# Gates turned to rows by a transpose, transposes of the rows in four later steps, and held weights at the last token blocks

## The chip, the cores and the metric

The kernel runs on one core of a Trainium2 chip. The core has a matrix engine (TensorE, PE in the profile; PEld is its weight load), VectorE (DVE), ScalarE (ACT), GpSimd (POOL) and SyncE (SP), which here does nothing but issue transfers. Every transfer of this kernel goes through the one queue that SP issues to. The metric is the time of one execution on the device in microseconds; the time shown is a median of several runs.

## The reference

The input is x, 512 tokens by 2048 features, float32, and a conditioning vector c. Two layers follow each other. Both are sandwich-normalised and modulated: for each layer `mod = silu(c) @ ada_w + ada_b` is split into shift, scale and gate, and the layer adds `gate * rmsnorm(y, g_post)` to the stream.

- Layer one is an mLSTM mixer with 8 heads (key width 256, value width 512): one input product `h @ w_in` gives queries, keys, values, an output gate o and a gate z; queries and keys go through a causal convolution of width 4; the head's output is normalised, multiplied with `sigmoid(o)` and `silu(z)`, and goes through `w_out` (4096 to 2048).
- From the residual stream after layer one, with its own norm and modulation (`kv_ada_w`), one shared set of keys and values is made: `kv = hkv @ kv_w`.
- Layer two is a band attention with 16 heads of width 128 and a relative-position bias. Its queries and a gate z come from `h @ b_w_in`; its output goes through `b_w_out` (2048 to 2048).

```
mod = sc @ ada_w[l] + ada_b[l]
shift, scale, gate = mod[:, :D], mod[:, D:2*D], mod[:, 2*D:]
h = modulate(rmsnorm(x, g_pre[l]), shift, scale)
...
x = x + gate[:, None, :] * rmsnorm(y, g_post[l])
```

## The kernel before

**Products.** Every large product is done in three matmuls on two halves of each operand: a float32 value is split into a rounded high part and the rest (`split`, L152: ScalarE casts the high part, L153; VectorE subtracts, L154). `mm3` (L176) issues high by high, high by low and low by high. Weights come as a stream of pieces in a fixed order (`wpiece`, L158): SP loads a raw piece of up to 512 KB (L167), then ScalarE and VectorE split it. Raw, high and low pieces have three buffers each, and this work has a priority `AHEAD` over what the program says at that place, so the planner puts it ahead of other work on each engine. `proj_a` (L192) keeps the weights stationary; `proj_b` (L195) keeps the tokens stationary, with two 128-row slices of 512 weight columns in a piece, for up to four blocks of 128 tokens: 24 matmuls a piece with four blocks, 12 with two. Sums lie in PSUM, five buffers for the large products (`newp`) and three for small ones (`newa`).

**Order.** A planner orders the instructions of each engine from the order of the program and its priorities. The loads and sums of the modulation are pinned to the program's order.

**Modulation.** `mod` has 128 columns of 128 values. Each column is two loads of 512 KB (`ada_load`, L236) and two multiply-and-sum instructions on VectorE (`ada_sum`, L240). The first 64 halves are done at the start, for what layer one needs first. The other 192 are done beside the heads: `background` (L401) sums the three halves that are loaded and then loads the next three, since there are three buffers. It is called in each head after the second and fourth of the query and key products (q1, q3), halfway through and behind the value product (vm, v), after the second and fourth o product (o1, o3), the same for z (z1, z3), and at the head's end; head 0 makes three of these calls, head 1 leaves the q calls out. What is left is summed after the last head.

**Layer one's end.** The gates (`gate` times the post-norm weight) are made as columns in `ggate` and stored to a scratch buffer `ggd` in one transfer (L538). `gate_row` (L567) reads 512 gate values of it, spread over all partitions, into the one buffer `gb`, which shares its memory with a buffer that the heads use. Each head leaves its normalised rows in the scratch buffer `ysc` by four stores (L526); `y_tile` loads them (L557, `yr`) and splits them for the output product. `rows` (L640) does that product: first column group 0 for all four token blocks, then groups 1 to 3 for the pair of blocks 0 and 1, then groups 1 to 3 for blocks 2 and 3. `evac` (L571) multiplies with the gate row and sums squares.

**Residual and transposes.** For each token block, `residual` (L583) finishes the post-norm, adds x, sums squares again and stores the rows; `turned` (L604) scales the rows by the new norm (`xn`, L613), transposes them in 128 by 128 blocks on TensorE (`ps_x`, L621), eight for a column group of a pair, keeps them (ScalarE, a store), and for the second pair makes the key inputs at once (`key_input`, L594). The first pair's residual and transposes happen in `rows(1, (2, 3))`; the second pair's come right after the last `rows`, at high priority, ahead of the value products `values` (L663).

```
with tc.high_priority(AHEAD):
    residual(2)
    residual(3)
    turned(1, True)
```

**Layer two's end.** The output product `b_w_out` takes three column groups with all four token blocks, then the last group for blocks 0 and 1, then for blocks 2 and 3 (L806 to L815). `finish` (L799) makes a block's norm factor, four final products (L803) and four stores (L804); blocks 0 and 1 finish during the last pair's product, blocks 2 and 3 after it.

Of the kernel before, what the change touches and what calls it, by code (L numbers as in the profile page):

```python
# [15 lines left out]
P = 128  # L16
D = 2048
S = 512
# [87 lines left out]
def hybrid_trunk(ctx, tc, xT, xN, c, adaT, cols, wst, wg, ext, kc, out):  # L106
# [88 lines left out]
    def proj_b(mat, xs, pss, midway=None, ms=range(4), kts=KT, at={}):  # L195

        for k0 in range(0, kts, 2):
            if midway and k0 == kts // 2:
                midway()
            if k0 in at:  # L200
                at[k0]()
            hi, lo = wpiece(mat)
            for j in range(2):
                k = k0 + j
                x = xs(k) if callable(xs) else xs[k]
                w = slice(j * 512, (j + 1) * 512)
                for ps, m in zip(pss, ms):
                    t = slice(m * P, (m + 1) * P)
                    mm3(ps, x[:, 0, t], x[:, 1, t], hi[:, w], lo[:, w], k == 0, k == kts - 1)
# [191 lines left out]
    def background(h=NH, where=""):  # L401

        if h == 0 and where not in ("vm", "v", "end") or h == 1 and where[0] == "q":
            return
# [5 lines left out]
        del pending[:ADA_BUFS]  # L410

    for h in range(NH):
# [27 lines left out]
        proj_b("a_w_in", h1, pv, lambda: background(h, "vm"))  # L440
# [86 lines left out]
        if h < NH - 1:  # L527
            background(h, "end")
    while loaded or pending:
        background()  # L530
    for k in range(KT):
        amul_col(KT + k, 96 + KT + k, KVG + k)
        amul_col(2 * KT + k, 48 + KT + k, GPRE + KT + k)
    nc.vector.tensor_tensor(ggate[:, :KT], mod[:, 2 * KT : 3 * KT], cl[:, GPOST : GPOST + KT], op=ALU.mult)
    nc.vector.tensor_tensor(
        ggate[:, KT:], mod[:, 48 + 2 * KT : 48 + 3 * KT], cl[:, GPOST + KT : GPOST + 2 * KT], op=ALU.mult
    )
    nc.sync.dma_start(ggd.rearrange("l k p -> p (l k)"), ggate)  # L538
# [44 lines left out]
    def residual(m):  # L583
        rs = row_rstd(m)
        for g in range(4):
# [6 lines left out]
            nc.sync.dma_start(xsc[m, :, d], y)  # L592

# [10 lines left out]
    def turned(pair, use):  # L604
# [3 lines left out]
        rs = [row_rstd(m) for m in ms]  # L608
        for g in range(4):
            xn = []  # L610
            for i, m in enumerate(ms):
                n = tp.tile([P, S], F32, tag="t", name=f"xn{m}_{g}")
                nc.vector.tensor_scalar(n, yt[m][g], rs[i], None, op0=ALU.mult)  # L613
# [36 lines left out]
    for pair, ms in enumerate(PAIRS):  # L650
        for g in range(1, 4):
            at = {}
            if pair == 1 and g == 1:
                at = {2: lambda: residual(0), 4: lambda: residual(1), 12: lambda: turned(0, False)}
# [15 lines left out]
    with tc.high_priority(AHEAD):  # L670
        residual(2)
        residual(3)
        turned(1, True)
    for ms in PAIRS:
        for g in range(2):
            values(g, ms)
# [129 lines left out]
    for g in range(4):  # L806
        gate_row(1, g)
        for pair in [range(4)] if g < 3 else PAIRS:
            ps = [newp(f"ps_y1_{g}_{m}") for m in pair]
            at = {4: lambda: finish(0), 6: lambda: finish(1)} if pair == PAIRS[1] else {}  # L810
            proj_b("b_w_out", y2, ps, ms=pair, at=at)
# [64 lines left out]
```

## Time and profile before

| | |
|---|---|
| median of 3 runs | 2883.31 us (2882.78 to 2885.15) |
| the profiled execution's own time | 2881.31 us |
| its span, first to last instruction | 2879.5 us |
| mean granted TensorE clock | 0.996 |
| data moved | 491.09 MB, mean 171 GB/s |
| weight loads of 512 KB | 520, median 3.3 us from issue to landing |
| modulation loads of 512 KB | 256, 5.6 us |
| loads of normalised rows (yr) | 16, 5.1 us |
| gate store `ggd<-ggate`, 16 KB | 1, 17.1 us |
| gate read-backs `ssum<-ggd`, 256 KB | 11, 3.5 us |

The span is that of the profiled execution; 1.81 us of its time lie around the span. Busy shares count the time in which an engine worked; a TensorE that is busy 99% can still start its matmuls further apart than the shortest pitch. A line of waits names the engine and the operation that waited, what released it, the sum of the waits, their number and the longest one. In a timeline the columns are the start, the length, the engine, the line, the operation and, in brackets, the idle time before it and what ended it. A granted clock of 1.00 is full speed; at half of it a 512-column matmul takes nearly twice as long.

### The profile page before, as it was taken

How to read it: one execution, taken by the hardware profiler on the slowest of the kernel's cores; microseconds unless marked ns; L12 is line 12 of the kernel's file. 1: busy time of each engine (PE TensorE's matmuls, PEld its weight loads, DVE VectorE, ACT ScalarE, POOL GpSimd, SP SyncE). 2: the span in 40 equal slices, each digit the busy share in tenths (PEclk: the TensorE clock that was granted, in tenths of full speed). 3: DMA queues.
4: the chain of work that ended last, by engine and by line, in shares of the span. 5: the costliest groups of instructions: out<-in, count | busy, mean ns of one | idle time of the engine just before them, and what ended most of it. 6: DMA issues, size and time to landing. Idle time of an engine off the chain costs nothing.

```text
span 2879.5 us, 33007 instructions
## 1 busy us (share of the span) xinstructions
PE 2839.1 (99%) x12768; PEld 2343.9 (81%) x12768; DVE 1587.6 (55%) x2358; ACT 1122.6 (39%) x1642; POOL 0.2 (0%) x4
## 2 busy tenths in 40 slices
PE   8999999999999999999999999999999999999998
PEld 5887888888888888888888788878888888888886
DVE  7985846475374664754646445575222455545425
ACT  4244534334242342422433345464222455545323
POOL 0000000000000000000000000000000000000000
PEclk9999999999999999999999999999999999999999
DMA  8874546455465454554546757686222322222334
GB/s 301 313 242 151 191 153 202 160 181 191 140 202 174 164 186 160 171 195 148 197 156 232 174 194 237 222 271 219 100 95 99 136 91 92 88 92 89 135 106 168
DMA packets 158998, 491.09 MB, mean 171 GB/s; under 512 B 21092, under 2 KB 30180, under 8 KB 158328
## 3 DMA queue, kind: packets, MB, share of 16 engines
q1 hardware_dynamic: 158840, 488.98, 50.5%
q8 instruction: 100, 1.64, 0.2%
q14 instruction: 58, 0.48, 0.0%
HBM read 467.89 MB, written 26.26 MB: 172 GB/s over the span
## 4 chain that ended last, share of the span: by engine, by line
PE 93%; DMA 3%; DVE 2%; ACT 1%; issue 1%; SPq 0%; DVEq 0%; ACTq 0%
PE ps_z L174 17%; PE ps_y L174 16%; PE ps_o L174 12%; PE ps_v L174 12%; PE ps_qk L174 9%; PE ps_q L174 6%; PE ps_k L174 6%; PE ps_kv L174 5%; PE ps_l L174 3%; PE ps_s L174 2%; PE ps_lead L174 2%; PE ps_n L174 2%; DMA yr<-ysc 1%; DVE wl L154 1%; PE ps_t L744 1%; DMA ada<-in_adaT 1%
## 5 line engine op out<-in xcount | busy, mean ns | idle before, releaser
L154 DVE TENSOR_TENSOR wl<-wr,wh 128x1024 fp32r<-128x1024 f32 (+3 forms) x586 | 680.3, 1162 | 1107.1 <-ACT wh L153 1106.5
L153 ACT CAST wh<-wr 128x1024 fp32r<-128x1024 f32 (+3 forms) x586 | 587.6, 1003 | 1439.1 <-PE ps_y L174 230.3
L174 PE MATMUL ps_y<-wh,y 128*128 128x512 f32 x1536 | 476.7, 391 | 7.1 <-ACT y L153 6.7
L174 PE MATMUL ps_z<-h,wh 128*128 128x512 f32 x1408 | 433.8, 389 | 0.0
L174 PEld LDWEIGHTS ps_y<-wh,y 128*128 128x128 f32 x1536 | 289.1, 189 | 68.1 <-ACT y L153 7.5
L174 PE MATMUL ps_v<-wh,h 128*128 128x512 f32 x1024 | 317.2, 389 | 0.0
L174 PEld LDWEIGHTS ps_z<-h,wh 128*128 128x128 f32 x1408 | 263.4, 188 | 54.0
L174 PE MATMUL ps_y<-wl,y 128*128 128x512 f32 x768 | 300.3, 391 | 0.0
L174 PE MATMUL ps_o<-h,wh 128*128 128x512 f32 x896 | 276.3, 389 | 0.0
L174 PE MATMUL ps_z<-h,wl 128*128 128x512 f32 x704 | 274.1, 389 | 0.0
L174 PE MATMUL ps_qk<-h,wh 128*128 128x512 f32 x768 | 237.7, 391 | 0.0
L174 PEld LDWEIGHTS ps_v<-wh,h 128*128 128x128 f32 x1024 | 192.1, 188 | 39.8
L174 PE MATMUL ps_v<-wl,h 128*128 128x512 f32 x512 | 199.5, 390 | 0.0
L174 PEld LDWEIGHTS ps_o<-h,wh 128*128 128x128 f32 x896 | 167.5, 188 | 34.3
L174 PE MATMUL ps_o<-h,wl 128*128 128x512 f32 x448 | 174.5, 389 | 0.0
L240 DVE CUSTOM_DVE_ANT_0 ada<-ada,scB,cl 128x1024 f32<-128x1024 f32 x128 | 163.9, 1281 | 13.4 <-DMA ada<-in_adaT 13.3
L240 DVE CUSTOM_DVE_ANT_0 ada<-ada,scB,mod 128x1024 f32<-128x1024 f32 x128 | 164.1, 1282 | 11.6 <-DMA ada<-in_adaT 10.2
L174 PEld LDWEIGHTS ps_y<-wl,y 128*128 128x128 f32 x768 | 144.8, 189 | 29.9
L174 PEld LDWEIGHTS ps_qk<-h,wh 128*128 128x128 f32 x768 | 143.3, 188 | 29.0
L174 PE MATMUL ps_kv<-wh,hkv 128*128 128x512 f32 x512 | 160.3, 393 | 0.0
L174 PE MATMUL ps_q<-h,wh 128*128 128x512 f32 x512 | 159.3, 392 | 0.0
L174 PE MATMUL ps_k<-hkv,wh 128*128 128x512 f32 x512 | 157.7, 389 | 0.0
(214 smaller groups left out, 3388.8 us busy)
## 6 DMA issues: line engine op xcount, KB each, us to landing
wr<-in_wst SPq DMA_DIRECT2D x520, 512.0 KB, 3.3
ada<-in_adaT SPq DMA_DIRECT2D x256, 512.0 KB, 5.6
yr<-ysc SPq DMA_DIRECT2D x16, 512.0 KB, 5.1
wr<-in_wst SPq DMA_DIRECT2D x30, 256.0 KB, 4.1
ysc<-so SPq DMA_DIRECT2D x28, 256.0 KB, 5.6
wr<-in_wst SPq DMA_DIRECT2D x16, 384.0 KB, 5.7
bsc<-in_ext SPq DMA_DIRECT2D x16, 320.0 KB, 5.8
xt<-in_xT SPq DMA_DIRECT2D x4, 1024.0 KB, 6.9
```

The lines of the kernel that those rows point to most:

```text
L153: nc.scalar.copy(hi, src)
L154: nc.vector.tensor_tensor(lo, src, hi.bitcast(F32), op=ALU.subtract)
L174: nc.tensor.matmul(ps, a, b, start=start, stop=stop)
L240: pin(nc.vector.tensor_tensor_reduce(at, at, scB[:, j * D // 2 : (j + 1) * D // 2], 1.0, mod[:, i : i + 1] if j else col(CB + i), ALU.mult ...
L744: nc.tensor.transpose(ps[:, P * (i - j) : P * (i - j + 1)], pr[i][:, P * j : P * (j + 1)], ident)
```

## The change

It has four parts.

1. `background` is called at pieces 4 and 10 of the value product instead of at piece 8. Head 0 uses one of the two (v4); head 1 leaves out q1, q3 and v4; the last head leaves out o3, z1 and z3. By the instruction order, heads 2 to 6 issue 30 loads each (27 before), the last head 15 (27 before), and no modulation load or sum is left after it.
2. `gates_out(layer)` replaces the one store of all gates. It multiplies the layer's 16 gate columns, transposes them on TensorE to 16 rows of 128 values, copies these on ScalarE, and stores rows of 512 bytes. Layer one's gates go out after head 3, layer two's after the last head.
3. `proj_b` goes through its last piece token block by token block, where before each 128-row slice went through all blocks. With `late=3`, which only the very last product has, the last three pieces are held; block 2 goes through all three, and then block 3.
4. `residual` ends with the new norm's factor, which was the start of `turned`. `turned` takes a list of column groups. For the first pair they are placed at pieces k = 16, 20, 24 and 28 of `rows(1, (2, 3))` (all four at 12 before); for the second pair at k = 0, 4, 8 and 12 of the second value product, at that place's own priority (all four ahead of the first value product at high priority before).

```diff
@@ -192,21 +192,26 @@
     def proj_a(mat, xs, ps, t0=0, t1=S):
         proj(mat, xs, [ps], 8, 0, len(xs), len(xs) - 1, t0, t1)
 
-    def proj_b(mat, xs, pss, midway=None, ms=range(4), kts=KT, at={}):
-
+    def proj_b(mat, xs, pss, ms=range(4), kts=KT, at={}, late=0):
+
+
+        held = []
         for k0 in range(0, kts, 2):
-            if midway and k0 == kts // 2:
-                midway()
             if k0 in at:
                 at[k0]()
-            hi, lo = wpiece(mat)
-            for j in range(2):
-                k = k0 + j
-                x = xs(k) if callable(xs) else xs[k]
-                w = slice(j * 512, (j + 1) * 512)
-                for ps, m in zip(pss, ms):
-                    t = slice(m * P, (m + 1) * P)
-                    mm3(ps, x[:, 0, t], x[:, 1, t], hi[:, w], lo[:, w], k == 0, k == kts - 1)
+            held.append((k0, *wpiece(mat)))
+            if k0 >= kts - 2 * late and k0 < kts - 2:
+                continue
+            for group in [[pm] for pm in zip(pss, ms)] if k0 == kts - 2 else [list(zip(pss, ms))]:
+                for ka, hi, lo in held:
+                    for j in range(2):
+                        k = ka + j
+                        x = xs(k) if callable(xs) else xs[k]
+                        w = slice(j * 512, (j + 1) * 512)
+                        for ps, m in group:
+                            t = slice(m * P, (m + 1) * P)
+                            mm3(ps, x[:, 0, t], x[:, 1, t], hi[:, w], lo[:, w], k == 0, k == kts - 1)
+            held.clear()
 
     def newp(name):
         return psP.tile([P, S], F32, tag="p", name=name)
@@ -400,7 +405,9 @@
 
     def background(h=NH, where=""):
 
-        if h == 0 and where not in ("vm", "v", "end") or h == 1 and where[0] == "q":
+        if h == 0 and where not in ("v4", "v", "end") or h == 1 and where in ("q1", "q3", "v4"):
+            return
+        if h == NH - 1 and where in ("o3", "z1", "z3"):
             return
         for a in loaded:
             ada_sum(*a, tc.keep_in_program_order)
@@ -408,6 +415,17 @@
         for i, j in pending[:ADA_BUFS]:
             loaded.append(ada_load(i, j, ap_, ADA_BUFS, tc.keep_in_program_order))
         del pending[:ADA_BUFS]
+
+    def gates_out(layer):
+
+        gg = ggate[:, layer * KT : (layer + 1) * KT]
+        c0 = 48 * layer + 2 * KT
+        nc.vector.tensor_tensor(gg, mod[:, c0 : c0 + KT], cl[:, GPOST + layer * KT : GPOST + (layer + 1) * KT], op=ALU.mult)
+        ps = newa(f"ps_gg{layer}")
+        nc.tensor.transpose(ps[:KT, :P], gg, ident)
+        row = tp.tile([P, S], F32, tag="t", name=f"gg{layer}")[:KT, :P]
+        nc.scalar.copy(row, ps[:KT, :P])
+        nc.sync.dma_start(ggd[layer], row)
 
     for h in range(NH):
         for i in (2 * h, 2 * h + 1):
@@ -437,7 +455,7 @@
             nmd, nm.rearrange("p (a b) -> p a b", a=4), maskd.unsqueeze(1).to_broadcast([P, 4, P]), op=ALU.add
         )
         pv = [newp(f"ps_v{h}_{m}") for m in range(4)]
-        proj_b("a_w_in", h1, pv, lambda: background(h, "vm"))
+        proj_b("a_w_in", h1, pv, at={k: lambda k=k: background(h, f"v{k}") for k in (4, 10)})
         v = []
         for m in range(4):
             if m < 3:
@@ -526,16 +544,14 @@
             nc.sync.dma_start(ysc[h, :, i, :], so[i])
         if h < NH - 1:
             background(h, "end")
+        if h == 3:
+            gates_out(0)
     while loaded or pending:
         background()
     for k in range(KT):
         amul_col(KT + k, 96 + KT + k, KVG + k)
         amul_col(2 * KT + k, 48 + KT + k, GPRE + KT + k)
-    nc.vector.tensor_tensor(ggate[:, :KT], mod[:, 2 * KT : 3 * KT], cl[:, GPOST : GPOST + KT], op=ALU.mult)
-    nc.vector.tensor_tensor(
-        ggate[:, KT:], mod[:, 48 + 2 * KT : 48 + 3 * KT], cl[:, GPOST + KT : GPOST + 2 * KT], op=ALU.mult
-    )
-    nc.sync.dma_start(ggd.rearrange("l k p -> p (l k)"), ggate)
+    gates_out(1)
     hst.close()
     phA.close()
 
@@ -590,6 +606,7 @@
             nc.vector.scalar_tensor_tensor(y, y, rs, xr, op0=ALU.mult, op1=ALU.add)
             nc.scalar.activation(newa(f"sqx{m}_{g}"), y, AF.Square, accum_out=ssq[:, 4 * m + g : 4 * m + g + 1])
             nc.sync.dma_start(xsc[m, :, d], y)
+        row_rstd(m)
 
     def key_input(k, tmp, t):
 
@@ -601,16 +618,15 @@
             hkv.append(xp.tile([P, 2, S], F32R, tag="x", name=f"hkv{k}"))
         split(hkv[k][:, 0, t], hkv[k][:, 1, t], tmp)
 
-    def turned(pair, use):
+    def turned(pair, gs, use):
 
         ms = PAIRS[pair]
         t = slice(2 * P * pair, 2 * P * (pair + 1))
-        rs = [row_rstd(m) for m in ms]
-        for g in range(4):
+        for g in gs:
             xn = []
             for i, m in enumerate(ms):
                 n = tp.tile([P, S], F32, tag="t", name=f"xn{m}_{g}")
-                nc.vector.tensor_scalar(n, yt[m][g], rs[i], None, op0=ALU.mult)
+                nc.vector.tensor_scalar(n, yt[m][g], rsn[:, m : m + 1], None, op0=ALU.mult)
                 xn.append(n)
             for kk in range(2):
                 k = 4 * g + 2 * kk
@@ -651,7 +667,8 @@
         for g in range(1, 4):
             at = {}
             if pair == 1 and g == 1:
-                at = {2: lambda: residual(0), 4: lambda: residual(1), 12: lambda: turned(0, False)}
+                at = {2: lambda: residual(0), 4: lambda: residual(1)}
+                at |= {16 + 4 * i: lambda i=i: turned(0, [i], False) for i in range(4)}
             if pair == 1 and g == 3:
                 at = {k: lambda k=k: [key_input(i, kept(i, slice(0, 2 * P)), slice(0, 2 * P)) for i in range(k // 2 - 1, k // 2 + 1)] for k in range(2, 32, 4)}
             gate_row(0, g)
@@ -670,10 +687,10 @@
     with tc.high_priority(AHEAD):
         residual(2)
         residual(3)
-        turned(1, True)
-    for ms in PAIRS:
+    for pair, ms in enumerate(PAIRS):
         for g in range(2):
-            values(g, ms)
+            turn = {4 * i: lambda i=i: turned(1, [i], True) for i in range(4)} if pair == 0 and g == 1 else {}
+            values(g, ms, turn)
     for i in range(KT):
         ps = newp(f"ps_k{i}")
         proj_a("kv_w", hkv, ps)
@@ -808,7 +825,7 @@
         for pair in [range(4)] if g < 3 else PAIRS:
             ps = [newp(f"ps_y1_{g}_{m}") for m in pair]
             at = {4: lambda: finish(0), 6: lambda: finish(1)} if pair == PAIRS[1] else {}
-            proj_b("b_w_out", y2, ps, ms=pair, at=at)
+            proj_b("b_w_out", y2, ps, ms=pair, at=at, late=3 if pair == PAIRS[1] else 0)
             with tc.high_priority(AHEAD):
                 for p, m in zip(ps, pair):
                     yo[m].append(op.tile([P, S], F32, tag="o", name=f"yo{m}_{g}"))
```

## The prediction

> **What bounds the kernel now.** I read the busy shares and the clock row of the page first, then the waits of TensorE over the whole span, then the waits and the timeline of the SP queue around the two longest of them, and last the tail.
>
> ```profile
> PE 2839.1 (99%) x12768; PEld 2343.9 (81%) x12768; DVE 1587.6 (55%) x2358; ACT 1122.6 (39%) x1642; POOL 0.2 (0%) x4
> ```
> ```profile
> PE ps_lead L174 <- ACT h L219: 6.8, 3, 3.4
> PE ps_y L174 <- ACT y L153: 6.7, 1, 6.7
> ...
> PE ps_x L621 <- DVE xn L613: 3.5, 4, 1.3
> ...
> PE ps_q L174 <- ACT sp_q L153: 1.8, 1, 1.8
> ...
> PE ps_kv L174 <- DVE wl L154: 0.8, 1, 0.8
> ```
>
> TensorE is the bound: at full clock one 512-column matmul starts every 0.2267 us, and nearly all the span is that pitch. What an edit can win is the time in which matmul starts lie further apart. Counted from the starts, that is 35.5 us in the first 80 us (not touched), 13.0 between 1530 and 1640 (A, the first token product with the output weights), 3.9 between 1780 and 1820 (B, transposes of pair 0), 7.8 between 1915 and 1960 (C, transposes of pair 1), about 14 in the attention stage, and about 1 per mLSTM head, where no wait of TensorE is listed at all. Behind the last matmul there is a tail (D) of 11.1 us.
>
> A, the SP queue's waits between 1500 and 1700, its timeline, and the windows (columns: length, busy of PE, PEld, DVE, ACT, POOL, granted clock, DMA share, GB/s):
>
> ```profile
> SPq L569 <- DMA ggd<-ggate: 10.9, 1, 10.9
> ```
> ```profile
> 1592.42 0.43 SPq L538 DMA_DIRECT2D ggd<-ggate  x1
> ...
> 1598.19 0.33 SPq L167 DMA_DIRECT2D wr<-in_wst  x1
> 1609.51 0.32 SPq L569 DMA_DIRECT2D ssum<-ggd  x1
> 1609.92 0.38 SPq L557 DMA_DIRECT2D yr<-ysc  x1
> ```
> ```profile
> 1606.00:1613.00 7.00, 0.45 (x2) 0.03 (x1) 0.00 (x0) 0.51 (x1) 0.00 (x0) 0.86 0.72 120
> 1613.00:1618.00 5.00, 4.84 (x12) 3.78 (x13) 3.81 (x5) 3.03 (x6) 0.00 (x0) 0.51 0.78 275
> 1926.00:1932.00 6.00, 4.70 (x27) 3.71 (x26) 5.64 (x12) 3.93 (x7) 0.00 (x0) 1.00 0.88 290
> 1932.00:1938.00 6.00, 4.86 (x25) 3.23 (x23) 4.87 (x12) 5.93 (x18) 0.00 (x0) 1.00 0.42 146
> 1938.00:1942.00 4.00, 3.34 (x8) 2.67 (x9) 4.00 (x8) 1.76 (x5) 0.00 (x0) 0.59 0.78 257
> ```
>
> The gates go out in 4-byte elements: issued at 1592.42, landed 17.1 us later. Their read-back stands in the one queue in use and waits 10.9 us; the next load of normalised head rows (yr) stands behind it at 1609.92, and TensorE starves at 1606. After that gap the clock is 0.51. The last two rows show half clock at C too, behind the transposes.
>
> D, the tail:
>
> ```profile
> 2867.77 1.37 DVE L572 TENSOR_TENSOR yo<-ps_y,ssum 128x512 f32<-128x512 f32 x2 [5.17 <-PE ps_y L174]
> ...
> 2868.02 0.39 PE L174 MATMUL ps_y<-wh,y 128*128 128x512 f32 x1
> ...
> 2870.27 2.74 DVE L803 SCALAR_TENSOR_TENSOR yo<-yo,rsn,x 128x512 f32<-128x512 f32 x4
> ...
> 2873.12 2.74 DVE L803 SCALAR_TENSOR_TENSOR yo<-yo,rsn,x 128x512 f32<-128x512 f32 x4
> ```
>
> Both last token blocks end together, so eight final products of 0.67 us stand in a row on VectorE behind the last matmul.
>
> **Part by part, against the profiled run: 2881.31 us, of which 2879.5 span; the median of the runs is 2.0 above it.**
>
> *Gates by rows, and modulation sums moved (A).* Removed from A: the store in 4-byte pieces, and six modulation sums (1.28 us each) with their loads that now stand between 1567 and 1588 among the head rows' splits. In the changed kernel all 256 loads are issued and summed before the last head's rows go out: heads 2 to 6 carry 30 instead of 27, the last 15 instead of 27. Layer 0's gates leave after head 3, some 700 us before their read, which then waits only for the last use of the buffer, about 1539.7. In the queue's new order the read stands ahead of the last head's four stores; layer 1's store stands next to it, waits for a transpose and a copy (about 1546.4), and holds the queue until then; the first normalised store is then ready at about 1555 and the weight load behind it is needed at 1577, so 20 us cover it. If that cover went, a store as slow as today's (17.1) would just be absorbed.
> What goes, from the starts of the matmuls: the wait for the sum of squares 1.9 (no sums between the norm's steps on VectorE), 0.9 near 1589, 6.9 at 1606, 0.4 behind it, and ten matmuls at 0.427 instead of 0.227, 2.0: together 12.1. The new transpose of the gates, its copy and a shorter wait ahead of the norm's sum stay: 0.4. Bounds: 12.1 if nothing stays; if the queue's hold until 1546.4 starves TensorE as the 1606 wait did, 12.1 less 6.9 less 2.0 = 3.2. I take 11.7, near the upper end, since the walk through the rows finds 20 us of cover.
> The Trainium skill ("DMA: Bandwidth & Descriptors", Specifications) says that transfers under 512 bytes get less than the line rate, with a read-modify-write; the trace's 17.1 us for 16 KB agrees, beside 3.5 us for the 256 KB read-back. By that rule alone the new 512-byte rows would leave at line rate, and the sum would be the same.
>
> *More modulation work per head (2 to 6).* Three more loads and sums each: 3 x 1.28 = 3.8 us of VectorE, busy 732.5 of 1268 us there, and 1.5 MB, where DMA has a share of 0.52. Product v now has calls at two places instead of one. Hidden by the weight pieces held ahead: a sum waiting for its load delays the next piece's subtract, but the buffers hold a piece of 5.44 us more. In the trace of before sums wait 11 times in the heads, 2.5 us at most, and TensorE never does. Without the cover each late load costs its excess over 5.44; the slowest modulation load took 12.3. Bounds: -1 (the heads' small gaps close) to +2.5 (half a microsecond in each of five heads); I take 0, the value in the trace of before.
>
> *Transposes of pair 0 spread over four places (B).* Today three waits of 0.33, 0.29 and 1.37 = 2.0. Each group of eight (1.04 us) now has some 24 matmuls = 5.4 us ahead of it for two products of 0.48 on VectorE. The first stands at the same place as today and keeps about 0.3: gain 1.7, between 0 and 2.0.
>
> *Transposes of pair 1 inside the second value product (C).* Today waits of 1.46, 0.94, 0.85 and three short ones = 3.8, then eight matmuls at half clock, 1.6. The rest (2.4) is transposes and changes of shape, and stays. In the changed order TensorE has 24 matmuls between groups: 5.44 + 1.04 = 6.48 us a round. VectorE needs two xn (0.95), four scalings and four subtracts (3.0) and two weight subtracts (2.3): 6.24 a round. That is tight. Bounds: 5.4 if nothing waits; if each of four groups waits as long as the longest today (4 x 1.46 = 5.8), -0.4. It fits by 0.2 a round, with pieces prepared ahead, so I take 1.0 of new waits: gain 4.4.
>
> *Tail (D).* The last three pieces are held; block 2's 18 matmuls go first, so block 2 is complete 18 x 0.2267 = 4.1 us before the end. Its final products end at E+0.8 (E: end of the last matmul), then for block 3 come evacuation 0.7, square and read 0.8, reduce, root and reciprocal 0.8, four products 2.74, with gaps: the last ends at E+5.65, today at 2875.86 = E+7.45. Gain 1.8. Held buffers: piece 14's cast can start when piece 8 frees them (2860.09 in today's times), its two halves need 2.5 us, and block 2 reaches it at 2862.8: a margin of 0.2. Bounds: 2.5 if block 3 evacuates ahead of block 2's products, -0.7 if the piece is late by its own 2.5 us.
>
> Sum: 11.7 + 0 + 1.7 + 4.4 + 1.8 = 19.6. 2881.3 - 19.6 = 2861.7; with 2.0, a median of 2863.7.
>
> **Rivals.** (1) *VectorE becomes the bound in C and the shapes of B keep their waits*: A and D alone, 13.5, time 2869.8. For it: 5.64 of 6.00 us busy in the window from 1926. Against: that window also holds the residual sums, which are over before the new place.
> (2) *Transposes in groups stop the clock*: half clock came at 1938 after 12 us in which transposes and waits of 1.5 at most were mixed with matmuls. Were each of the eight groups followed by eight matmuls at half clock (1.6 each, 12.8, where today 1.6 is paid), the sum would be 19.6 - 12.8 = 6.8: 2876.5. Against: the 32 transposes of B show 1.00 throughout, and 1.04 us is shorter than any stretch that brought half clock here. The Trainium skill ("TensorE: Matmul & The Clock Gate", Part 4) says transposes do not count as work for the gate; C's half clock agrees, B's full clock shows a group alone is not enough.
> (3) *Slower: the sums in product v starve TensorE.* From the call ahead of product v to the first one in it, 10.9 us (two pieces) lie between loads and sums where there were 21.8; if loads land late, VectorE stands in order before the weight subtracts. It must cost 19.6 / 5 = 3.9 us a head to cancel all, and 5.1 a head for slower by 0.2%: 2863.7 + 5 x 5.1 = 2889.2. That takes a sum about 10 us late, past the 5.44 of cover. Against it, 2.5 us is the longest seen there.
> (4) *The change doesn't do what it says* (the planner draws the transposes together again): the instruction order shows them apart, so only a runtime wait could undo it; it falls in with (1).
>
> **How the numbers follow.** Forecast within its own bounds (2860 to 2868): 0.61. Rival 1 and partial forms of it: 0.18 (2868 to 2872). Rival 2: 0.07, just faster in 0.03 of it and the same in 0.04. Rival 3: 0.10, of which 0.03 stays within 0.2% and 0.07 is slower. Gains beyond my terms: 0.04. The range reaches from 2859 (12.1 + 1 + 2.0 + 5.4 + 2.5 = 23.0 would be 2860.3, a little run difference below) to 2872. 0.2% (5.8 us) is about what a measurement tells from no change here: faster 0.61 + 0.18 + 0.04 + 0.03 = 0.86, same 0.07, slower 0.07.
>
> **What would show it.** Right: no wait of the queue at the gate's read; waits of TensorE between 1530 and 1640 under 1.5 us, clock 1.00 there; waits before ps_x under 1.5 in all; last matmul to span end 9.3 us; no wait listed in the heads. Wrong: gaps of TensorE in product v of heads 2 to 6; half clock behind each group of transposes; a wait for the piece held last, about 4 us before the end.

## The result, and the profile after

The changed kernel takes 2863.37 us (median of 4 runs, 2862.53 to 2863.64) against 2883.05 of the kernel before (4 runs): ratio 0.993, with a 95% interval of 0.9913 to 0.9948, so a gain of 0.7% that is clear of no change. The forecast was 2863.7. The profiled execution took 2862.53 us with a span of 2860.7, so its span is 18.8 us shorter than before.

The first lines of the page, and TensorE's waits over the whole span (engine, operation, releaser: sum, number, longest):

```profile
PE 2832.2 (99%) x12770; PEld 2340.4 (82%) x12770; DVE 1587.4 (55%) x2358; ACT 1126.1 (39%) x1646; POOL 0.2 (0%) x4
```

```profile
PE ps_lead L174 <- ACT h L224: 7.8, 4, 3.4
...
PE ps_kv L174 <- DVE wl L154: 0.8, 1, 0.8
...
PE ps_x L637 <- DVE xn L629: 0.2, 1, 0.2
...
PE ps_x L637 <- DVE hkv L154: 0.2, 1, 0.2
```

The waits of 6.7 for the head rows (y) and of 1.8 for ps_q (the sum of squares of the last head's norm) are gone, and of the 3.5 before the transposes (ps_x) 0.4 is left. A wait of 0.8 for a weight half (wl) before ps_kv is listed as before, but at another place: it ends at 1914, in front of the transposes of the second pair, where it ended at 1939, behind them, in the kernel before. The same windows as before, and the whole stretch of the first row product (length, busy time of PE, PEld, DVE, ACT, POOL, granted clock, DMA share, GB/s):

```profile
1606.00:1613.00 7.00, 7.00 (x32) 5.81 (x31) 3.71 (x6) 3.10 (x5) 0.00 (x0) 1.00 0.48 156
1613.00:1618.00 5.00, 5.00 (x23) 4.13 (x22) 1.99 (x3) 1.76 (x3) 0.00 (x0) 1.00 0.66 210
1938.00:1942.00 4.00, 4.00 (x24) 3.27 (x23) 3.56 (x6) 2.27 (x5) 0.00 (x0) 1.00 0.80 281
1530.00:1640.00 110.00, 110.00 (x499) 91.42 (x498) 59.36 (x71) 46.41 (x70) 0.00 (x0) 1.00 0.58 197
```

TensorE is busy for all of the 110 us, and half clock is nowhere to be seen in these places. The heads show no wait of TensorE, as before. The queue's waits between 1480 and 1700 for what concerns the gates (L428 is the store of layer two's gate rows, L585 are the reads, each of which waits for the last use of the one buffer):

```profile
SPq L585 <- DVE y L588: 4.3, 2, 3.5
...
SPq L428 <- ACT gg L427: 3.2, 1, 3.2
...
SPq L585 <- DVE dd L520: 0.9, 1, 0.9
```

No read waits for a store any more. The store of layer two's gate rows holds the queue for 3.2 us, until 1547.41; TensorE shows no wait for it. The tail:

```profile
2849.29 2.74 DVE L820 SCALAR_TENSOR_TENSOR yo<-yo,rsn,x 128x512 f32<-128x512 f32 x4
...
2851.94 0.69 DVE L588 TENSOR_TENSOR yo<-ps_y,ssum 128x512 f32<-128x512 f32 x1
...
2854.10 2.74 DVE L820 SCALAR_TENSOR_TENSOR yo<-yo,rsn,x 128x512 f32<-128x512 f32 x4
```

Block 2's four final products start while block 3's matmuls still run (the last ends at 2851.17); block 3's evacuation follows behind them.

For what went where, I took the starts of the same matmul in both traces. A runs from the first matmul of the last head's ps_d to the end of the first row product (the start of the second), B is the row product of column group 1 for blocks 2 and 3, C runs from the first value product to the first key product, D from the end of the last matmul to the span's end.

| stretch | before, us | after, us | difference | forecast |
|---|---|---|---|---|
| span start to the last head's ps_d | 1534.96 | 1535.82 | +0.86 | 0 |
| A | 107.72 | 95.56 | -12.16 | -11.7 |
| B | 49.27 | 47.64 | -1.63 | -1.7 |
| C | 96.64 | 92.50 | -4.14 | -4.4 |
| D | 11.12 | 9.54 | -1.58 | -1.8 |
| all the rest | | | -0.16 | 0 |
| span | 2879.53 | 2860.71 | -18.8 | -19.6 |

Of the +0.86 at the start, 0.63 are there before the first value product. In the runs below, whose work up to there is that of one of these two kernels, the start of the first value product lies between 0.2 earlier and 2.6 later than in the trace of before, so it is the spread of executions. No term is far off. But the experiments show that the largest term, A, was right for a reason that was in part wrong.

### The profile page after: what moved, and what is told of

Read it like the earlier page. It is cut to its first block, busy times and chain, and to the rows that moved or that the text cites. A ratio compares the mean times of both kernels' runs of the same rounds, so it can differ in the third digit from the quotient of the medians.

```text
span 2860.7 us, 33028 instructions
## 1 busy us (share of the span) xinstructions
PE 2832.2 (99%) x12770; PEld 2340.4 (82%) x12770; DVE 1587.4 (55%) x2358; ACT 1126.1 (39%) x1646; POOL 0.2 (0%) x4
## 4 chain that ended last, share of the span: by engine, by line
PE 93%; DVE 3%; DMA 2%; issue 1%; ACT 1%; SPq 0%; DVEq 0%; ACTq 0%
PE ps_y L174 17%; PE ps_z L174 17%; PE ps_o L174 12%; PE ps_v L174 12%; PE ps_qk L174 9%; PE ps_q L174 6%; PE ps_k L174 6%; PE ps_kv L174 5%; PE ps_l L174 2%; PE ps_s L174 2%; PE ps_n L174 2%; PE ps_lead L174 1%; DVE wl L154 1%; DVE ada L245 1%; DMA wr<-in_wst 1%
```

## The experiments

Each group of runs has its own runs of the kernel before, on the same chip: 2884.59 us (median) beside e1 to e4, 2883.18 beside e5 to e8, 2884.97 beside e9 to e11, 2884.87 beside e12. Lengths of stretches come from the profiled executions, one for each kernel, as in the table. They have a spread of their own: in the traces whose edit leaves a stretch as the changed kernel has it, A lies between 95.5 and 96.5 us, B between 47.4 and 47.8, C between 92.4 and 93.3 (but 94.7 in e6) and D between 9.5 and 9.6. The intervals of the ratios are some 0.3% wide, about 9 us, so most of what follows rests on the stretches and on the waits in them.

### A: the gates and the modulation sums

**e1_old_store: the changed kernel with the old store of the gates.**

```diff
-        if h == 3:
-            gates_out(0)
...
-    gates_out(1)
+    nc.vector.tensor_tensor(ggate[:, :KT], ...)
+    nc.vector.tensor_tensor(ggate[:, KT:], ...)
+    nc.sync.dma_start(ggd.rearrange("l k p -> p (l k)"), ggate)
```

> The changed kernel with the gates stored the old way, in one transfer of 4-byte elements; the modulation sums stay moved. Theory (the store hurt because the late sums put it right ahead of its read): with the sums done early the planner can issue the store some 50 us ahead of the read, so its 17 us are hidden; TensorE waits between 1530 and 1640 stay under 1.5 us and the time is that of the changed kernel, 2863.4, within 1.5. Rival (the small elements cost wherever they stand): the queue waits for the store again, a gap of 5 to 7 us in TensorE with half clock behind it, 2870 to 2874.

Measured: 2864.2 us (2863.65 to 2864.62), ratio 0.9934 (0.9918 to 0.9951). A is 95.26 us long, 0.3 shorter than with gate rows. The queue's timeline, ScalarE's next late weight cast and two windows show where the store went:

```profile
1454.68 0.38 SPq L556 DMA_DIRECT2D ggd<-ggate  x1
1457.79 21.82 SPq L167 DMA_DIRECT2D wr<-in_wst  x5
```

```profile
1473.96 1.05 ACT L153 CAST wh<-wr 128x1024 fp32r<-128x1024 f32 x1 [6.81 <-DMA wr<-in_wst]
```

```profile
1456.00:1468.00 12.00, 12.00 (x55) 9.93 (x54) 3.54 (x4) 4.49 (x5) 0.00 (x0) 1.00 0.76 20
1530.00:1640.00 110.00, 110.00 (x499) 91.58 (x498) 59.37 (x72) 45.98 (x68) 0.00 (x0) 1.00 0.58 199
```

With the sums done early, the planner issues the store 87 us ahead of its read at 1541.5. For 12 us the core's transfers then run at 20 GB/s. The weight load issued right behind the store, at 1457.79, holds up ScalarE until 1473.96, so it took some 16 us here too; but TensorE is busy throughout, since pieces that had been loaded earlier covered it. (That five weight loads go out in 21.82 us is the usual pace of one in 5.44.) So the moved sums alone bring all of A's gain, and the new form of the gates adds nothing to it here: 0.3 is less than the spread of A.

**e2_old_sums: the changed kernel with the old places of the modulation calls.**

```diff
-        if h == 0 and where not in ("v4", "v", "end") or h == 1 and where in ("q1", "q3", "v4"):
-            return
-        if h == NH - 1 and where in ("o3", "z1", "z3"):
+        if h == 0 and where not in ("v8", "v", "end") or h == 1 and where[0] == "q":
             return
...
-        proj_b("a_w_in", h1, pv, at={... for k in (4, 10)})
+        proj_b("a_w_in", h1, pv, at={... for k in (8,)})
```

> The changed kernel with the old places of the modulation calls (27 halves a head, six sums left behind the last head); the gates still go out as rows, layer one's after head 3. Theory: the waits of 1.9 and 0.9 us that the sums made come back, the long gap near 1606 does not: +2.5 to +3.5 over the changed kernel, 2866 to 2867. Rival (the sums and their loads in the queue made the long gap themselves): +9 to +12, 2872 to 2875.

Measured: 2871.95 us (2870.12 to 2875.36), ratio 0.9962 (0.9948 to 0.9977): 8.6 over the changed kernel. The theory misses, and the time is near the rival's. A is 104.21 us, 8.65 longer. But its gap is not the old one, nor the one the rival named. TensorE's waits in this run, and two windows:

```profile
PE ps_gg L423 <- DVE ggate L421: 3.1, 1, 3.1
PE ps_y L174 <- ACT y L153: 1.7, 1, 1.7
PE ps_q L174 <- ACT sp_q L153: 1.2, 1, 1.2
```

```profile
1585.00:1589.00 4.00, 0.92 (x5) 0.42 (x3) 3.81 (x6) 0.00 (x0) 0.00 (x0) 1.00 0.09 36
1589.00:1593.00 4.00, 3.96 (x11) 3.17 (x12) 0.00 (x0) 0.26 (x1) 0.00 (x0) 0.57 0.35 133
```

The new transpose of layer two's gates stands on TensorE in front of ready matmuls and waits 3.1 us for the last sum; half clock follows.

**e3_rows_late: the old places of the sums, and one store of 32 rows of 512 bytes behind the last sum**, issued at 1590.08, ahead of its read at 1592.74.

```diff
-        ps = newa(f"ps_gg{layer}")
-        nc.tensor.transpose(ps[:KT, :P], gg, ident)
...
+        ps = newa("ps_gg")
+        nc.tensor.transpose(ps[: 2 * KT, :P], ggate, ident)
...
+        nc.sync.dma_start(ggd.rearrange("l k p -> (l k) p"), row)
```

> The changed kernel with the old places of the modulation calls, and with both layers' gates in one store behind the last sum, as in the kernel before, but as 32 rows of 512 bytes behind a transpose: the same place, other pieces. Theory (the 17.1 us landing of 4-byte elements is what starved TensorE): the store lands in about 3 us, the wait at its read is 3 to 5 us instead of 10.9, the gap near 1606 is under 1 us; +2.5 to +4 over the changed kernel, 2866 to 2867.5. Rival (the place of the store, not the pieces): the read still waits 8 us or more and the time is 2871 to 2875.

Measured: 2871.24 us (2869.2 to 2872.67), ratio 0.9958 (0.9943 to 0.9973). Neither forecast holds as it stands. The queue's wait at the read is short, shorter even than the 3 to 5 us of the first one:

```profile
SPq L581 <- DMA ggd<-gg: 2.3, 1, 2.3
```

The time is the rival's all the same:

```profile
PE ps_gg L423 <- DVE ggate L421: 2.0, 1, 2.0
PE ps_q L174 <- ACT sp_q L153: 2.0, 1, 2.0
PE ps_y L174 <- ACT y L153: 1.7, 1, 1.7
```

A is 103.72 us, with the transpose waiting 2.0 us for the last sum, half clock behind it (0.57 in the window from 1589.5 to 1593.5), and 1.7 us for head rows. Shortening the store's landing gave back 4.0 us of A's 12.2, and a new wait took the place of much of the old one.

**e5_columns_early: as e2, but without transposes: two stores of 4-byte elements**, 8 KB each, layer one's after head 3.

```diff
-        ps = newa(f"ps_gg{layer}")
-        nc.tensor.transpose(ps[:KT, :P], gg, ident)
-        row = tp.tile([P, S], F32, tag="t", name=f"gg{layer}")[:KT, :P]
-        nc.scalar.copy(row, ps[:KT, :P])
-        nc.sync.dma_start(ggd[layer], row)
+        nc.sync.dma_start(ggd[layer].rearrange("k p -> p k"), gg)
```

> As e2 (old places of the modulation sums), but without the transposes: each layer's gates leave in one store of 4-byte elements, layer one's after head 3, layer two's behind the last sum. Theory (in e2 and e3 the long loss came from the new transpose, which stood on TensorE in front of ready matmuls and waited 2 to 3 us for the last sum, with half clock behind it): the wait before ps_gg and the half clock go, and of the 8.6 us that e2 loses in the stretch of the first row product 2 to 4 remain: 2866 to 2868. Rival (the late sums and their loads starve the row loads by themselves): 7 us or more of loss remain, 2870 to 2873.

Measured: 2872.23 us (2871.27 to 2876.1), ratio 0.9965 (0.9952 to 0.9978); A is 103.08 us, 7.5 over the changed kernel. The theory's 2 to 4 us miss; the size is the rival's, but e9 will show that its cause (the late sums and their loads by themselves) is not. The wait before the transpose is gone and a gap for head rows is back, although no read waits for the store in this kernel:

```profile
PE ps_y L174 <- ACT y L153: 4.5, 1, 4.5
```

Its queue and ScalarE around the gap:

```profile
1593.25 0.43 SPq L422 DMA_DIRECT2D ggd<-ggate  x1
1596.06 2.03 SPq L567 DMA_DIRECT2D yr<-ysc  x1
```

```profile
1611.13 1.14 ACT L153 CAST y<-yr 128x512 fp32r<-128x512 f32 x2 [8.88 <-DMA yr<-ysc]
```

The row load issued right behind the store, at 1596.06, lands at 1611.1, 15.0 us later. With this, the trace of the kernel before reads differently. Its queue, ScalarE, and the chain of waits:

```profile
1592.42 0.43 SPq L538 DMA_DIRECT2D ggd<-ggate  x1
1595.31 2.71 SPq L557 DMA_DIRECT2D yr<-ysc  x1
```

```profile
1612.49 1.14 ACT L153 CAST y<-yr 128x512 fp32r<-128x512 f32 x2 [13.64 <-DMA yr<-ysc]
```

```profile
1590.84 21.63 DMA yr<-ysc x2
```

The load that ScalarE waited for until 1612.47 was issued at 1595.31, ahead of the read, and took 17.2 us, not the one at 1609.92 behind the read. The transfers of the kernel before in the window from 1575 to 1620, in 40 slices of 1.125 us:

```profile
GB/s 339 404 426 393 299 291 204 346 415 295 62 11 0 36 328 215 153 167 368 145 6 1 5 33 7 33 84 55 36 36 36 62 277 362 413 222 284 175 269 233
```

From slice 21 (1597.5) to slice 32 (1611) the queue moves between 1 and 84 GB/s: the 4-byte store, which lands at 1609.49, is being worked off, and what was issued behind it waits. The weight load behind it, at 1598.19, took 15.6 us as well.

**e9_gates_later: as e2, with layer two's gate rows only behind the first row product.**

```diff
-    gates_out(1)
...
     rows(0, range(4), y_tile)
+    gates_out(1)
```

> As e2 (old places of the modulation sums, layer one's gate rows out after head 3), with layer two's gates made and stored only behind the first row product, so that neither a transpose nor a store of gates stands near the late sums. What is left in that stretch is the price of the late sums and their loads alone. Theory (late sums cost the wait for the sum of squares and little else): 1 to 3.5 us over the changed kernel, 2864.5 to 2867. Rival (the sums' loads alone hold VectorE, then the weight pieces and the row loads behind them): a wait of TensorE of 1.5 us or more near 1590 remains, with half clock if it is over 3, 2868 to 2872.

Measured: 2865.38 us (2864.22 to 2866.85), ratio 0.9931 (0.9917 to 0.9945). TensorE's waits in A:

```profile
PE ps_q L174 <- ACT sp_q L153: 1.2, 1, 1.2
...
PE ps_n L174 <- DVE so L533: 0.4, 1, 0.4
```

A is 97.50 us, 1.9 over the changed kernel and 1.0 over the longest A of the traces that leave A alone. So the late sums alone cost 1 to 2 us: the theory holds, near its lower end, and nothing of the rival's 1.5 us near 1590 is listed. The time of the whole kernel agrees but can't show so little by itself.

**e12_late_store_alone: the changed kernel, with layer two's gates in one 4-byte store that falls into the first row product.** The gates are made to depend on a tile of head rows (times zero), so that the store comes late; no read is near.

```diff
-    gates_out(1)
...
-    rows(0, range(4), y_tile)
+    def late_store():
+        gg = ggate[:, KT:]
+        nc.vector.tensor_tensor(gg, mod[...], cl[...], op=ALU.mult)
+        nc.vector.scalar_tensor_tensor(gg, ys[17][:, 0, :KT].bitcast(F32), 0.0, gg, op0=ALU.mult, op1=ALU.add)
+        nc.sync.dma_start(ggd[1].rearrange("k p -> p k"), gg)
+
+    rows(0, range(4), y_tile, {18: late_store})
```

> The changed kernel (sums early, layer one's gate rows early), but layer two's gates leave in one store of 4-byte elements, 8 KB, that is made to wait for a tile of head rows and so falls into the first row product, near 1590, as the store of the kernel before did; no read waits for it. Theory (it is the store that holds up the loads issued behind it, not the read's wait in the queue and not the late sums): the row load behind it lands after 12 to 15 us, TensorE waits 3 to 5 us for it with half clock behind, 4.5 to 7 us over the changed kernel, 2868 to 2870.5. Rival (without the late sums the pieces are far enough ahead to cover it): the load lands as late, but TensorE waits less than 1 us, within 1.5 of 2863.4.

Measured: 2868.11 us (2867.74 to 2869.12), ratio 0.9944 (0.9927 to 0.996), 4.7 over the changed kernel, at the theory's lower end; A is 100.64 us, 5.1 longer. The size is right, the form is not. The queue:

```profile
1579.05 0.47 SPq L669 DMA_DIRECT2D ggd<-ggate  x1
1580.04 2.31 SPq L167 DMA_DIRECT2D wr<-in_wst  x1
```

The weight load right behind the store landed after 14.4 us, and the next row load, issued at 1588.74, after 7.1. There is no long gap and no half clock; the pieces arrive late one after the other, and TensorE loses 0.3 to 1.0 us at each of six starts. Waits in this run:

```profile
PE ps_y L174 <- DVE wl L154: 1.5, 4, 0.8
...
PE ps_y L174 <- ACT wh L153: 0.7, 1, 0.7
```

Not all of the 5.1 is the store's: 0.7 is a wait before ps_q, ahead of the store, that e6, e8, e10 and e11 list at 0.5 to 0.8 without any late store. So I counted, from 1560 to 1650, what the matmul starts lose against the shortest pitch:

| kernel | sums | layer two's gates | lost from 1560 to 1650, us |
|---|---|---|---|
| before | late | one 16 KB store with layer one's, 4-byte elements | 10.1 |
| e5 | late | 8 KB store, 4-byte elements | 6.1 |
| e12 | early | 8 KB store, 4-byte elements, made late | 4.4 |
| e9 | late | rows, behind this product | 0.3 |
| changed, e1 | early | stored before 1560 | 0.0 |

A late store of 4-byte elements is common to the three large losses, with late sums or early ones; late sums without it lose 0.3 here, and the rest of their 1 to 2 us ahead of 1560, in the norm's steps. Of the 3.9 us between the kernel before and e5, it was not separated what the second 8 KB and what the read's wait of 10.9 us make.

A likely reason why this product has so little cover, argued from the kernel's text and not tested: its head rows (yr) and its weight pieces (wr) share the three raw buffers, and each piece of work needs one of both, where the heads, in which e1's store fell, load weight pieces alone through them.

### B and C: the transposes

**e4_old_turns: the changed kernel with the transposes in their old places.**

```diff
-                at |= {16 + 4 * i: lambda i=i: turned(0, [i], False) for i in range(4)}
+                at |= {12: lambda: turned(0, range(4), False)}
...
     with tc.high_priority(AHEAD):
         residual(2)
         residual(3)
+        turned(1, range(4), True)
...
-            turn = {4 * i: lambda i=i: turned(1, [i], True) for i in range(4)} if pair == 0 and g == 1 else {}
-            values(g, ms, turn)
+            values(g, ms)
```

> The changed kernel with the transposes in their old places: pair 0's all at piece 12 of the third row product, pair 1's all behind the residuals, ahead of the first value product at high priority. Theory: the 1.6 of B and the 4.1 of C come back, half clock behind the second burst: +5 to +7 over the changed kernel, 2868.5 to 2870.5. Rival (the gain in C is from another source, the earlier stages' timing): under +2.5.

Measured: 2869.41 us (2868.42 to 2870.49), ratio 0.9952 (0.9938 to 0.9967): 6.0 over the changed kernel, as the theory said. B is 48.76 us, 1.1 longer, and C 97.81, 5.3 longer. Half clock is back, though not where the kernel before has it: here it follows a wait of 2.2 us for the rows (xn) early in the burst, and none is seen behind the last transposes:

```profile
1915.00:1919.50 4.50, 2.28 (x12) 1.78 (x11) 3.02 (x5) 2.90 (x6) 0.00 (x0) 0.84 0.80 264
1919.50:1922.00 2.50, 2.50 (x8) 2.00 (x8) 2.35 (x7) 2.25 (x5) 0.00 (x0) 0.60 0.76 261
```

**e7_one_burst: all of pair 1's transposes called at once, at ordinary priority.**

```diff
-            turn = {4 * i: lambda i=i: turned(1, [i], True) for i in range(4)} if pair == 0 and g == 1 else {}
+            turn = {4: lambda: turned(1, range(4), True)} if pair == 0 and g == 1 else {}
```

> The changed kernel with all four column groups of pair 1's transposes called at once, at piece 4 of the second value product, still at ordinary priority. Theory (what mattered is that the weight pieces go ahead of them on VectorE, not the list of four places): the planner spreads them over about 110 matmul rows by itself, the stretch of the first two value products stays within 1.5 us of the changed kernel's, 2862.5 to 2865. Rival (the burst itself stalls TensorE): waits of 3 us or more before ps_x, half clock behind them, 2867 to 2869.

Measured: 2863.94 us (2862.8 to 2866.89), ratio 0.9937 (0.9922 to 0.9952). C is 92.13 us, as with four places, and no wait before ps_x is listed. In its trace 24 to 29 value matmuls stand between one group and the next: the planner spreads them once the weight pieces go ahead of them. So the gain in C doesn't come from the four calls, but from leaving the high priority or from the later place, inside the second value product; these two were changed together, and no run separates them. It also means that this run does not show what a real burst at that place would cost.

**e10_residuals_inside: the second pair's residuals inside the first value product, at ordinary priority.**

```diff
-    with tc.high_priority(AHEAD):
-        residual(2)
-        residual(3)
...
+            if pair == 0 and g == 0:
+                turn = {2: lambda: residual(2), 4: lambda: residual(3)}
```

It was aimed at the wait that C kept. In the changed kernel, ScalarE around it:

```profile
1911.42 0.60 ACT L607 ACTIVATE sqx<-y 128x512 f32<-128x512 f32 x1 [2.02 <-DVE y L606]
1911.96 0.19 ACT L607 ACTIVATION_READ_ACCUMULATOR sqx<-y 128x1 f32 x1
1912.05 1.03 ACT L153 CAST wh<-wr 128x1024 fp32r<-128x1024 f32 x1
```

> The changed kernel with the second pair's residuals called at pieces 2 and 4 of the first value product, at ordinary priority, instead of ahead of it at high priority. Theory (the wait of 0.8 us for a weight half near 1913 comes from ScalarE, which stands at high priority at the squares of rows that wait for their x loads, in front of the next weight cast): that wait goes, 0.8 to 1.2 us faster in the stretch of the first two value products, 2862 to 2863. Rival (the weight load itself is late there, whatever the order): the wait stays, within 0.4 of the changed kernel.

Measured: 2862.81 us (2862.47 to 2863.06), ratio 0.9922 (0.9908 to 0.9935). C is 91.20 us, 1.3 shorter than in the changed kernel, and the wait for the weight half is gone; what is listed in C is one wait of 0.2 before ps_x. The theory holds: the square that waited 2.02 us for its rows stood in front of a weight cast that shows no other wait. In the time of the whole kernel, 0.6 us below the changed one in another group of runs with overlapping ratios, this can't be told from no change.

### Heads

**e8_tight_sums: the two modulation calls in the value product at pieces 6 and 8.**

```diff
-        proj_b("a_w_in", h1, pv, at={... for k in (4, 10)})
+        proj_b("a_w_in", h1, pv, at={... for k in (6, 8)})
```

> The changed kernel with the two modulation calls in the value product at pieces 6 and 8 instead of 4 and 10, so that loads have 10.9 us where they had 16.3. Theory (a sum that waits a little for its load is covered by the weight pieces held ahead, one piece is 5.44 us): the waits of VectorE for modulation loads in the heads grow from 25.7 to 40 to 60 us in all, TensorE shows no wait there, time within 1.0 of the changed kernel. Rival (there was little cover left): 0.5 to 3 us a head, 2866 to 2880.

Measured: 2863.41 us (2862.61 to 2865.3), ratio 0.9934 (0.9919 to 0.9949). TensorE has no wait in the heads:

```profile
262.00:1530.00 1268.00, 1267.57 (x5722) 1054.52 (x5721) 744.01 (x1011) 460.84 (x583) 0.00 (x0) 1.00 0.53 177
```

VectorE's waits for modulation loads hardly grow, against what I expected: 27.0 us in all, 25.7 in the changed kernel. So the time part of the theory holds and its 40 to 60 us of waits do not: the sums hardly come to lean on the cover.

### D: the tail

**e6_no_hold: the changed kernel without held pieces.**

```diff
-            proj_b("b_w_out", y2, ps, ms=pair, at=at, late=3 if pair == PAIRS[1] else 0)
+            proj_b("b_w_out", y2, ps, ms=pair, at=at)
```

> The changed kernel with no pieces held for the very last product (its last piece alone still goes block by block). Theory: block 2 ends 6 matmuls, 1.4 us, before the end instead of 4.1, so its final products again stand in front of block 3's; the stretch from the last matmul to the span's end grows from 9.5 to 10.5 to 11.1 us, time +1.0 to +1.6, 2864.4 to 2865. Rival (the last stores, not VectorE, set the end): under +0.4.

Measured: 2866.35 us (2866.11 to 2867.68), ratio 0.9945 (0.9928 to 0.9962), 3.0 over the changed kernel. The tail is 11.13 us again, 1.6 longer: the held pieces are all of D's gain, and taking the last piece block by block is worth nothing. The time grew by more than that, past the 2865 expected. The rest lies in C, 94.65 us, 2.2 longer, where a second weight half was late and half clock followed (0.52 between 1916 and 1919). The program there is that of the changed kernel. ScalarE's square in front of the weight cast, the one that e10 moves, waited 3.17 us for its rows here instead of 2.02; why the rows came later was not tried, and stays open.

**e11_tail_split: as e10, with two of block 2's final products on ScalarE and GpSimd.**

```diff
-            nc.vector.scalar_tensor_tensor(y, y, rs, x2[m][g], op0=ALU.mult, op1=ALU.add)
+            if m == 2 and g < 2:
+                nc.scalar.activation(y, y, AF.Copy, scale=rs)
+                nc.gpsimd.tensor_tensor(y, y, x2[m][g], op=ALU.add)
+            else:
+                nc.vector.scalar_tensor_tensor(y, y, rs, x2[m][g], op0=ALU.mult, op1=ALU.add)
```

> As e10, with two of block 2's four final products done as a scaling on ScalarE and an addition on GpSimd. Theory (block 3's evacuation stands 0.8 us behind block 2's last final product on VectorE): the stretch from the last matmul to the span's end falls from 9.5 to 8.7 or 8.8 us, time 0.8 below e10. Rival (GpSimd's additions or their stores end last): the stretch stays or grows past 9.5.

Measured: 2862.7 us (2861.62 to 2864.22), ratio 0.9922 (0.9909 to 0.9936). The tail is 9.05 us, 0.5 below e10's 9.56, where 0.8 was expected. GpSimd's two additions take 2.96 us and end before block 3's products do:

```profile
2850.54 2.96 POOL L821 TENSOR_TENSOR yo<-yo,x 128x512 f32<-128x512 f32 x2 [2850.10 <-ACT yo L820]
...
2853.81 2.74 DVE L823 SCALAR_TENSOR_TENSOR yo<-yo,rsn,x 128x512 f32<-128x512 f32 x4
```

In the time of the whole kernel it doesn't show beside e10.

## Why the prediction was right, point by point

**The method.** Counting what TensorE loses against its shortest pitch, stretch by stretch, gave the size of what was to be won. All four terms came within 0.5 us: 11.7 against 12.2, 1.7 against 1.6, 4.4 against 4.1, 1.8 against 1.6. Rival 1 (A and D alone) and rival 2 (half clock behind each group) did not come about: B and C gained, and the clock is 1.00 in the windows of C that were read, from 1905 to 1946. Rival 3 fell: the heads are without a wait, even with the calls moved closer (e8). Rival 4 did not come about either: the groups stand apart in the trace, and the planner spreads them even when they are called at once (e7).

**A: the sum was right, one step of its mechanism was wrong.** The prediction said that the row load stands in the queue behind the gates' read, at 1609.92, "and TensorE starves at 1606". The load that TensorE waited for had been issued at 1595.31, ahead of the read and behind the store. The store held up the transfers behind it, whether or not a read waited: e5 has no such wait and a gap of 4.5 us, e12 none and a loss of 4.4. That the number came right all the same is partly luck: the edit removed the late store and the read behind it together, so the whole loss went, whichever of them had made it.

A second point was left together: the 6.9 and 2.0 us were counted under both edits of A, the gates by rows and the moved sums, without saying which of them removes the loss. By the experiments the new form of the gates was not what gave this gain, and would not have been enough. With the sums left late, rows leave 8.2 to 8.7 us of the 12.2 in place (e2, e3), since their transpose waits on TensorE for the last sum. With the sums done early, the old store costs nothing (e1); the prediction's remark that a store as slow as today's would just be absorbed pointed the same way. The lower bound given for A, a gain of 3.2, was close to what e2 would have brought (107.72 - 104.21 = 3.5), but by chance, since another wait than the one named for it made it. What pays in A is that nothing of the modulation is left behind the last head: the sums' own 1 to 2 us, and the time that it gives the gates to leave.

The Trainium skill ("DMA: Bandwidth & Descriptors", Specifications) puts the line-rate limit at 512 bytes; the landings agree, 17.1 us for 16 KB in 4-byte elements and 1.3 us for 8 KB in rows of 512 bytes in the changed kernel. It prices the transfer itself, and e1 shows that this price alone need not matter.

**C: the size was right, the place of what was left was not.** I took 1.0 us of new waits because VectorE is nearly full in the rounds of transposes (6.24 of 6.48 us). In the changed kernel it is just as full there:

```profile
1932.00:1938.00 6.00, 6.00 (x32) 5.03 (x31) 6.00 (x13) 4.06 (x8) 0.00 (x0) 1.00 0.80 262
```

VectorE is busy for all of the 6.00 us, and so is TensorE. What was left of the 5.4, 1.3 us, lies earlier, at 1913, where matmul starts lose 1.3 us before a weight half that ScalarE was late with; e10 moved its cause and won 1.3 us. So the term was nearly right in size by an offset: among the transposes a single wait of 0.2 us is listed, and a loss that was not foreseen stands ahead of them.

**D: a little too much.** I had the last final product at 5.65 us behind the last matmul; it ended at 2854.10 + 2.74 = 2856.84, which is 5.67 behind. The remaining 3.87 us to the span's end were 2879.53 - 2875.86 = 3.67 in the kernel before. So the walk was right and the last store's end was mis-sized by some 0.2. For the piece held last no wait of TensorE is listed, so the margin of 0.2 us was enough.

## What to carry to other kernels

Before a slow transfer's own time is counted, look at what was issued behind it in the same queue: find the transfer that ended the wait by its issue time, not by the nearest line that waits. A step that is only needed for a later stage (here sums, and what depends on the last of them) is best finished ahead of a stage with little cover; where it can't be, a new form of it can bring a new wait, on the engine that does it, as the transposes did in e2 and e3. And an edit with several parts can be right as a whole when one part would have been enough: undo them one by one before copying all of them.

## What the runs showed of the hardware

- A store in 4-byte elements held up what was issued behind it in the same queue: 16 KB landed after 17.1 us (before), 8 KB after 13.1 (e5). Loads of 512 KB issued right behind them took 17.2 us (before), 15.0 (e5) and 14.4 (e12), where the medians in the kernel before are 3.3 us for weights and 5.1 for rows, and the core's transfers ran at 1 to 84 GB/s meanwhile (before).
- Half clock needed no long pause of TensorE, and the pause's length alone did not decide it. In e3 the matmul starts around the transpose of the gates lay 2.4 us apart, and the clock was 0.57 in the next 4 us; in the same trace the starts before ps_q lay 2.4 us apart as well, and the clock stayed at 1.00. In the kernel before, a wait of 1.8 us before ps_q was followed by none. The Trainium skill ("TensorE: Matmul & The Clock Gate", What's actually happening) gives an idle window of some 3.4 us, running freely; the pause in e3 was shorter than that, and the measurement decides.
- GpSimd took 1.5 us on average for an addition of 128x512 float32 values (2.96 for two, e11), where VectorE's final product of the same shape takes 0.7 (2.74 for four).
